# Leftover blocks of a mixture of experts: each down projection moved behind the next block's ups and row turns, and the loads past the end of the list put under conditions

## The chip, the cores and the metric

The kernel runs on one core of one Trainium2 chip. A core has engines with queues of their own: PE (TensorE, matrix products and transposes), DVE (VectorE), ACT (ScalarE), POOL (GpSimd) and SP (SyncE, which here only issues transfers), and 16 DMA engines that move data between the chip's memory (HBM) and the on-chip buffers. Engines work through their own instructions in order and wait for each other by semaphores. The metric is the device time of one execution in microseconds (us); a measurement is the median of several.

## The reference, cut to what matters

One layer of a hybrid decoder trunk over 512 tokens of 1024 values: three token mixers in parallel, then a mixture of experts (64 routed experts, 8 for each token, and one shared), all in 32-bit floats. The change touches only the routed experts:

```python
def block_step(acc, inp):
    tok, wt, e = inp                      # up to 128 tokens of one expert
    xb = x_pad[tok]                       # gather the rows
    hb = jax.nn.silu(xb @ w1[e]) * (xb @ w3[e])      # ups: 1024 -> 2 x 256
    yb = (hb @ w2[e]).astype(jnp.float32) * wt[:, None]   # down: 256 -> 1024
    return acc.at[tok].add(yb), None      # add into the tokens' rows
```

## The kernel before

Routing gives every expert a list of tokens. The kernel sorts the lists into blocks. Full pairs of blocks go first, in a nest of conditions of its own (`n_four`, 8 rounds in this input). What is left goes through `block(i)`, one expert's block of up to 128 tokens at a time. The number of such blocks, `n_left`, is known only at run time (9 here), so `block` is written out 96 times, each time inside one more `tc.If(n_left > i)`: every engine compares and falls into the next block, or jumps out of the nest. The order of the instructions on each engine is the order in which the code is written (`tc.manual_schedule()`); the queues run against each other only by semaphores.

One block i, as it stands in the code:

- **Loads (SP).** `load_up` brings the two up matrices of block i+2, 1 MB each, into `ra[i%2]` (L1006, L1008); `load_down` (L1012) brings its down matrix, 1 MB, into `rad[i%2]`. Blocks past the end of the list have an entry too, so the last two blocks load matrices that nobody uses.
- **Ups (PE, L1153 to L1155).** 24 matmuls: the rows and the weights are each split into a rounded part and the rest (`mT_hi`, `mT_lo`; `wh`, `wl`), and three products of four are summed. While they run, ACT (L49) and DVE (L50) split the next block's weights (`split_a`), in four parts; the last part follows the ups.
- **Activation.** ACT's Silu (L1162), DVE's product with the token's weight, `hw` (L1163).
- **Row turns (PE, L1146).** `x_a` transposes the gathered rows `xg` of the next block, and ACT and DVE split them into `mT_hi` and `mT_lo`.
- **Turns of hw (PE, L1278).** `turn_b` transposes `hw`; ACT copies the result into `hb` (L1280).
- **Down (PE, L1288).** `down_b`: 8 matmuls into two banks `py`; DVE scales each half into `y` (L1289).
- **Row numbers.** `ia[i%2]` holds a block's row numbers and weights. `slots` (DVE, L1133) copies them to `sa`, a tile with two buffers, so that POOL may overwrite `ia` for block i+2 (L1118) and gather that block's rows (L1120).
- **Add (POOL, L1191).** `add_a` sends `y` by an indirect transfer that adds it to the rows `sa` of `acc2` in HBM (the trace names it `acc`). A tile that such a transfer reads is free when the transfer has landed.

After the nest, the sum is read back from HBM in four parts on ACT's and SP's queues (L1378), joined with what the first stage had summed (L1379), normalised and written.

Of the kernel before, what the change touches and what calls it, by code (L numbers as in the profile page):

```python
# [9 lines left out]
F32 = mybir.dt.float32  # L10
F32R = mybir.dt.float32r
BF = mybir.dt.bfloat16
I32 = mybir.dt.int32
AF = mybir.ActivationFunctionType
OP = mybir.AluOpType
# [3 lines left out]
IOA = bass.IndirectOffsetOnAxis  # L19

P = 128
D = 1024
S = 512
# [4 lines left out]
E = 64  # L28
# [6 lines left out]
def trunk(ctx, tc, x, c, ada_w, ada_b, norm1, norm2, w_in, conv_a_w, conv_a_b, ln_a_g, ln_a_b,  # L35
# [4 lines left out]
    nc = tc.nc  # L40
    V, A, G, T = nc.vector, nc.scalar, nc.gpsimd, nc.tensor
    dbg = dbg or {}
    x, out = x[0], out[0]
# [33 lines left out]
    h2d = dram.tile([S, D], F32, name="h2d")  # L77

    acc, acc2 = (dram.tile([S, D], F32, name=n) for n in ("acc", "acc2"))
# [12 lines left out]
    hT = (big.tile([P, KT, S], F32R, name="hT_hi"), big.tile([P, KT, S], F32R, name="hT_lo"))  # L92
# [86 lines left out]
    for i in range(4):  # L179
        a = sp.tile([P, KT, 2, 256], F32, name="ada", bufs=3)  # L180
# [84 lines left out]
    xg = shifted(pl[1], 13, "xg", big)  # L265
# [562 lines left out]
    row, ti = hp.tile([P, TT, 8, 2], F32, name="row"), hp.tile([P, TT, 8], I32, name="ti")  # L828
# [3 lines left out]
    def rt(shape, name, dt=F32, bufs=1, tag=None):  # L832
        return hp.tile([P] + shape, dt, name=name, bufs=2 if tag in ("x1", "h2", "tm", "hf2") else bufs, tag=tag or name)
# [102 lines left out]
    for ts in ((0, 1), (2,), (3,)):  # L936
# [7 lines left out]
        for t in ts:  # L944
# [18 lines left out]
            for g2, q in enumerate(halves):  # L963
# [7 lines left out]
                for i in range(4):  # L971
                    k = g2 * 4 + i
# [18 lines left out]
    ew = est.enter_context(tc.tile_pool(name="ew", bufs=1, side="right"))  # L991
# [11 lines left out]
    def load_up(raw, row, j, after=None):  # L1003
        e = nc.sync.value_load(first[0:1, j:j + 1] if row is None else items[0:1, row, j:j + 1], min_val=0, max_val=E - 1)
        up = raw[j % 2]
        i = nc.sync.dma_start(up[:, :2048], w1v[:, ds(e, 1)].rearrange("p e f -> p (e f)"))  # L1006
        sync_after(i, after)
        nc.sync.dma_start(up[:, 2048:], w3v[:, ds(e, 1)].rearrange("p e f -> p (e f)"))  # L1008

    def load_down(raw, row, j):  # L1010
        e = nc.sync.value_load(first[0:1, j:j + 1] if row is None else items[0:1, row, j:j + 1], min_val=0, max_val=E - 1)
        nc.sync.dma_start(raw.rearrange("p (k f) -> p k f", k=2), w2v[:, ds(e, 1)].rearrange("p e k f -> p (e k) f"))  # L1012
# [19 lines left out]
    V.scalar_tensor_tensor(cls[:, 1], svf, 64.5, cls[:, 2], op0=OP.is_lt, op1=OP.mult)  # L1032
    for j in range(2):
        V.tensor_tensor_scan(cum[:, j], ones, cls[:, j], (2.0, 0.0)[j], op0=OP.mult, op1=OP.add)
    nn_, mi = rt([2], "nn_"), rt([3], "mi", I32)
    V.scalar_tensor_tensor(mi[:, 0:1], cum[:, 0, P - 1:], 31.0, cum[:, 1, P - 1:], op0=OP.min, op1=OP.min)
    V.tensor_scalar(mi[:, 1:2], mi[:, 0:1], 1, None, op0=OP.logical_shift_right)
    V.tensor_scalar(nn_[:, 0:1], mi[:, 1:2], 2.0, None, op0=OP.mult)
# [8 lines left out]
    V.tensor_tensor(L[:, 0], cls[:, 2], lf[:, 0], op=OP.subtract)  # L1047
    V.tensor_tensor_scan(cl_, ones[:, 0:1].to_broadcast([P, 2 * P]), L.rearrange("p a e -> p (a e)"), nn_[:, 1:2], op0=OP.mult, op1=OP.add)
    V.tensor_copy(mi[:, 2:3], cl_[:, 2 * P - 1:])
    it, jk2, th = rt([5], "it"), rt([2 * P], "jk2", tag="tm"), rt([1], "th")  # L1050
    V.scalar_tensor_tensor(jk2[:, :P], cum[:, 0], iop, ones, op0=OP.is_le, op1=OP.mult, accum_out=it[:, 0:1])
    V.scalar_tensor_tensor(jk2[:, :P], cum[:, 1], iop, ones, op0=OP.is_le, op1=OP.mult, accum_out=it[:, 1:2])
# [22 lines left out]
    items = ew.tile([1, 7, P], I32, name="items")  # L1075
    iv = items[:, 0:6].rearrange("o (b a) e -> o a b e", a=2)
    V.memset(items[:, 6], 0)
    for a, src in enumerate((v_, c_)):
# [1 line left out]
        for j in range(3):  # L1080
            T.matmul(ips[:, j], src[:, j:j + 1], ident, start=True, stop=True)
        V.tensor_copy(iv[:, a], ips)
    V.tensor_copy(items[:, 6, 0:2], mi[0:1, 1:3])
    hst.close()
    rawst.close()


    n_four = nc.values_load(items[0:1, 6, 0:1], min_val=0, max_val=15)
    n_left = nc.values_load(items[0:1, 6, 1:2], min_val=0, max_val=NL)
    ep = est.enter_context(tc.tile_pool(name="ep", bufs=1))  # L1090
    psx = est.enter_context(tc.tile_pool(name="psx", bufs=1, space=PSUM))
    xg = [ep.tile([P, D], F32, name=f"xg{b}") for b in range(2)]
# [22 lines left out]
    def gather_a(row, j, n=2):  # L1115
        s = j % 2
        cl = G.value_load(items[0:1, row + 1, j:j + 1], min_val=0, max_val=4 * E - 1)
        G.tensor_copy(ia[s], idxw[:, ds(cl, 2)])  # L1118
        for b in range(n):
            G.indirect_dma_start(out=xg[b], out_offset=None, in_=h2d, in_offset=IOA(ap=ia[s][:, b, 0:1], axis=0),  # L1120
                                 bounds_check=S - 1, oob_is_err=False)

    def gather_c(row, j):
        s = j % 2
# [6 lines left out]
    def slots(src, shape, name):  # L1131
        t = ep.tile([P] + shape, I32, name=name, bufs=2)
        V.tensor_copy(t, src)  # L1133
        return t

    def split_a(j, u, up=None):
        if u < 4:
            src = (up or ra[j % 2]).rearrange("p (z k f) -> p k z f", z=2, k=KT)[:, 2 * u:2 * u + 2]
            split(*(w[u].rearrange("p (k z f) -> p k z f", k=2, z=2) for w in (wh, wl)), src)
        else:  # L1140
            split(wh[u], wl[u], rad[j % 2][:, (u - 4) * 1024:(u - 3) * 1024])

    def x_a(b, g):
        pt = psx.tile([P, 4, P], F32, name="pt", bufs=2)
        for k in range(4):
            T.transpose(pt[:, k], xg[b][:, (g * 4 + k) * P:(g * 4 + k + 1) * P], ident)  # L1146
        split(h2T[0][b][:, g * 4:g * 4 + 4], h2T[1][b][:, g * 4:g * 4 + 4], pt)
# [42 lines left out]
    def add_a(y, at, beside=None, to=acc):  # L1190
        st = G.indirect_dma_start(out=to, out_offset=IOA(ap=at, axis=0), in_=y, in_offset=None,  # L1191
                                  compute_op=OP.add, bounds_check=S - 1, oob_is_err=False)
        g = beside or f"run {st.ins.name}"
        if beside:
            tc.declare_no_dep(st.ins, group=g, reason="the rows of a run are distinct")
        tc.add_to_no_dep_group(g, st.ins)
        return g
# [77 lines left out]
    def turn_b(hw):  # L1275
        p3 = pse.tile([P, 2, 2, P], F32, name="p3")
        for k in range(2):
            T.transpose(p3[:, 0, k], hw[:, k * P:(k + 1) * P], ident)  # L1278
        hb = ew.tile([P, 2, P], F32, name="hb", tag="hh")
        A.activation(hb, p3[:, 0], AF.Copy)  # L1280
        return hb

    def down_b(i, hb):
        y = ew.tile([P, D], F32, name="y", bufs=2)
        for h in range(2):
            py, q = pse.tile([P, 512], F32, name="py", bufs=2), slice(h * 512, h * 512 + 512)
            for k in range(2):
                T.matmul(py, hb[:, k], rad[i % 2][:, k * 1024 + h * 512:k * 1024 + h * 512 + 512], start=(k == 0), stop=(k == 1))  # L1288
            V.tensor_tensor(y[:, q], py, gm2[:, q], op=OP.mult)  # L1289
        return y  # L1290

    def block(i):
        if i:
            load_up(ra, GL, i + 2)
        up = rc[0] if i == 1 else None
        ph = ps_up((0,))
        for u in range(4):
            up_a(ph, u)
            if u < 3:
                split_a(i + 1, u, up)  # L1300
        hw = act_a(ph[0], ia[i % 2][:, 0, 1:2])
        sa = slots(ia[i % 2], [2, 2], "sa")
        split_a(i + 1, 3, up)
        x_a(0, 0)
        x_a(0, 1)
        hT = turn_b(hw)
        gather_a(GL, i + 2, 1)
        add_a(down_b(i, hT), sa[:, 0, 0:1], to=acc2)
        load_down(rad[i % 2], GL, i + 2)

    gs, tok = rad[1][:, :D], ew.tile([P, TT], I32, name="tok")
    nc.sync.dma_start(gs, modr[3:4].to_broadcast([P, D]))
# [25 lines left out]
    with tc.manual_schedule():  # L1338
        gather_a(GA, 0)
        copied = gather_c(GC, 0)  # L1340
        for t in range(2):
            run = add_a(ysh[t], tok[:, t:t + 1], run)
        load_up(rc, GC, 0, copied)
        load_down(rcd, GC, 0)
        for g in range(4):
            x_a(g // 2, g % 2)
        gather_a(GA, 1)
        nc.sync.dma_start(fn[0:1], final_norm[None, :])
        A.activation(gm2, gs, AF.Copy)
        for z in range(2):  # L1350
            zq = slice(z * CH, z * CH + CH)
            A.activation(gm2c[zq], gs[zq, z * 512:z * 512 + 512], AF.Copy)
        for t in range(2, TT):
            run = add_a(ysh[t], tok[:, t:t + 1], run)
        for u in range(6):
            split_a(0, u)
        load_down(rad[1], GA, 1)
        with ExitStack() as nest:
            for i in range(15):
                nest.enter_context(tc.If(n_four > i))  # L1360
                pair_of_runs(2 * i)
                pair_of_runs(2 * i + 1)

        nc.scalar.dma_start(rc[1].rearrange("p (t d) -> p t d", t=TT), acc.rearrange("(t p) d -> p t d", p=P))
        for h in range(2):
            py, q = pse.tile([P, 512], F32, name="py", bufs=2), slice(h * 512, h * 512 + 512)
            T.matmul(py, ones[0:1], fn[0:1, q], start=True, stop=True)
            A.activation(fn[:, q], py, AF.Copy)
        with ExitStack() as nest:  # L1369
            for i in range(NL):  # L1370
                nest.enter_context(tc.If(n_left > i))
                block(i)


    fs = ew.tile([P, TT], F32, name="fs")
# [41 lines left out]
```

## Time and profile before

| | before |
|---|---|
| median of 3 runs | 1465.79 us (1462.84 to 1471.63) |
| the profiled execution | 1467.86 us, span 1466.1 us |
| mean granted clock of PE | 0.966 of full speed |
| leftover stage | first up 1328.65, last `y` ends 1437.9, reads of the sum from 1445.6 |
| distance of one leftover block from the next | 11.86 us |

All times of the profile count from the start of the span. The span is what lies between the first and the last instruction; the execution's time is 1.8 us longer. A row of a timeline gives start, length, engine, line, operation and tiles, and in square brackets how long the engine stood idle before it and what ended that. `PEld` is the loading of a matmul's fixed operand, which overlaps PE; a `q` behind an engine's name stands for its sequencer (branches, semaphores, issuing of transfers).

### The profile page before, as it was taken

What the parts mean: (1) busy time and instruction counts of PE and PEld (TensorE: products, weight loads), DVE (VectorE), ACT (ScalarE), POOL (GpSimd) and SP (SyncE); (2) the same over time, 40 slices, a digit from 0 to 9 for tenths busy, and PEclk for the clock granted to TensorE, in tenths of its full rate; (3) what the DMA queues carried; (4) which work ended last, traced back from release to release, by engine and by line L of the source; (5) the groups of instructions that cost most, each with busy time, mean ns of one, the idle gap of its engine ahead of it and who ended that gap; (6) DMA issues with size and microseconds to landing.
All of it is one profiled execution on the core that took longest, in us unless ns stands there. A gap on an engine that the chain in (4) does not pass through costs nothing. (4 is left out here: it accounts for less than half of the span.)

```text
span 1466.1 us, 24089 instructions
## 1 busy us (share of the span) xinstructions
PE 1347.5 (92%) x8982; PEld 968.7 (66%) x8982; DVE 956.0 (65%) x1816; ACT 620.3 (42%) x1019; POOL 264.8 (18%) x255
## 2 busy tenths in 40 slices
PE   4999999999999979998998978999999999997881
PEld 3877777776766756664686635777677777774660
DVE  6865998987777777233455855666656566564664
ACT  4454334427568658220212213434434443443442
POOL 1000000000000000000000354243342524333332
PEclk8999999999999989999999989999999999999996
DMA  9321231232112117759826348999898989966985
GB/s 339 110 58 31 66 89 47 69 125 92 31 59 80 31 51 237 242 185 333 278 74 238 134 154 266 371 341 322 322 313 294 314 301 337 321 219 206 317 285 208
DMA packets 120634, 289.13 MB, mean 197 GB/s; under 512 B 14883, under 2 KB 68397, under 8 KB 109486
## 3 DMA queue, kind: packets, MB, share of 16 engines
q1 hardware_dynamic: 99266, 242.87, 46.2%
q0 software_dynamic: 17904, 36.01, 10.0%
q10 hardware_dynamic: 3324, 8.49, 1.6%
q8 instruction: 75, 1.23, 0.3%
q14 instruction: 65, 0.53, 0.1%
HBM read 260.24 MB, written 46.97 MB: 210 GB/s over the span
## 5 line engine op out<-in xcount | busy, mean ns | idle before, releaser
L53 PE MATMUL ps_in<-hT_hi,w_hi 128*128 128x512 f32 x496 | 203.9, 411 | 2.7 <-ACT hT_hi L49 2.7
L54 PE MATMUL ps_in<-hT_hi,w_lo 128*128 128x512 f32 x496 | 201.5, 406 | 0.3 <-DVE w_lo L50 0.2
L55 PE MATMUL ps_in<-hT_lo,w_hi 128*128 128x512 f32 x496 | 199.9, 406 | 0.0
L50 DVE TENSOR_TENSOR wl<-ra,wh 128x1024 fp32r<-128x1024 f32 x100 | 122.1, 1224 | 115.2 <-ACT wh L49 111.6
L49 ACT ACTIVATE wh<-ra 128x1024 fp32r<-128x1024 f32 x100 | 105.6, 1060 | 127.8 <-PE ph L1155 90.0
L1153 PE MATMUL ph<-wh,mT_hi 128*128 128x512 f32 x328 | 134.5, 410 | 2.3 <-ACT wh L49 2.3
L1154 PE MATMUL ph<-wl,mT_hi 128*128 128x512 f32 x328 | 129.6, 395 | 0.5 <-DVE wl L50 0.5
L1155 PE MATMUL ph<-wh,mT_lo 128*128 128x512 f32 x328 | 129.3, 394 | 0.0
L50 DVE TENSOR_TENSOR w_lo<-w_raw,w_hi 128x1024 fp32r<-128x1024 f32 x76 | 92.5, 1223 | 51.0 <-ACT w_hi L49 50.8
L53 PEld LDWEIGHTS ps_in<-hT_hi,w_hi 128*128 128x128 f32 x496 | 94.6, 191 | 34.3 <-issue 7.6
L1191 POOL DMA_INDIRECT acc<-y,sa x41 | 65.6, 1599 | 272.9 <-DVE hc L1227 238.0
L54 PEld LDWEIGHTS ps_in<-hT_hi,w_lo 128*128 128x128 f32 x496 | 94.4, 190 | 21.7 <-issue 1.7
L55 PEld LDWEIGHTS ps_in<-hT_lo,w_hi 128*128 128x128 f32 x496 | 94.3, 190 | 21.8 <-issue 2.7
L49 ACT ACTIVATE w_hi<-w_raw 128x1024 fp32r<-128x1024 f32 x76 | 79.3, 1052 | 38.8 <-PE ps_p L55 18.3
L594 DVE SCALAR_TENSOR_TENSOR u<-ut,par,u 128x512 f32<-128x512 f32 x120 | 84.2, 747 | 0.6
L70 POOL TENSOR_TENSOR h<-h,mhalf 128x4 f32<-128x4 f32 x8 | 10.5, 1310 | 358.4 <-DVE h L393 358.4
L1153 PEld LDWEIGHTS ph<-wh,mT_hi 128*128 128x128 f32 x328 | 62.7, 191 | 18.2 <-issue 3.4
L1154 PEld LDWEIGHTS ph<-wl,mT_hi 128*128 128x128 f32 x328 | 62.8, 191 | 15.3 <-issue 1.9
L1155 PEld LDWEIGHTS ph<-wh,mT_lo 128*128 128x128 f32 x328 | 62.6, 191 | 13.3
L1187 DVE TENSOR_TENSOR y<-py,rows 128x512 f32<-128x512 f32 x64 | 44.1, 689 | 31.9 <-PE py L1185 25.1
L49 ACT ACTIVATE wh<-rad 128x1024 fp32r<-128x1024 f32 x34 | 34.1, 1050 | 71.8 <-issue 36.1
L1120 POOL DMA_INDIRECT xg<-h2d,ia x45 | 56.3, 1250 | 20.3 <-issue 8.8
(523 smaller groups left out, 2754.5 us busy)
## 6 DMA issues: line engine op xcount, KB each, us to landing
ra<-in_exp_w_dram SPq DMA_DIRECT2D x52, 1024.0 KB
rc<-in_exp_w_dram SPq DMA_DIRECT2D x34, 1024.0 KB
w_raw<-in_w_in_dram SPq DMA_DIRECT2D x31, 1024.0 KB
rad<-in_exp_w_dram SPq DMA_DIRECT2D x27, 1024.0 KB
adar<-in_ada_w_dram SPq DMA_DIRECT2D x32, 512.0 KB
rcd<-in_exp_w_dram SPq DMA_DIRECT2D x16, 1024.0 KB
ada<-in_ada_w_dram SPq DMA_DIRECT2D x8, 1024.0 KB
gd<-sg SPq DMA_DIRECT2D x24, 256.0 KB
```

Of the source, the lines that this page charges most:

```text
L49: A.activation(hi, src, AF.Copy)
L50: (lo_engine or V).tensor_tensor(lo, src, hi.bitcast(F32), op=OP.subtract)
L53: T.matmul(ps, l[0], r[0], start=first, stop=False)
L54: T.matmul(ps, l[1], r[0], start=False, stop=False)
L55: T.matmul(ps, l[0], r[1], start=False, stop=last)
L594: V.scalar_tensor_tensor(u[:, ct], ut[ct][:, w:w + S], col("caw", w * 4 + ct), u[:, ct], op0=OP.mult, op1=OP.add)
L1120: G.indirect_dma_start(out=xg[b], out_offset=None, in_=h2d, in_offset=IOA(ap=ia[s][:, b, 0:1], axis=0), bounds_check=S - 1, oob_is_err=False)
L1153: T.matmul(ph[b], h2T[0][b][:, k], wh[u][:, q], start=(k == 0), stop=False)
L1154: T.matmul(ph[b], h2T[0][b][:, k], wl[u][:, q], start=False, stop=False)
L1155: T.matmul(ph[b], h2T[1][b][:, k], wh[u][:, q], start=False, stop=(k == KT - 1))
L1187: V.tensor_tensor(y[:, q], py, gate[:, q], op=OP.mult)
L1191: st = G.indirect_dma_start(out=to, out_offset=IOA(ap=at, axis=0), in_=y, in_offset=None, compute_op=OP.add, bounds_check=S - 1, oob_is_er ...
```

## The change

The down projection of block i-1 is written behind the ups and the row turns of block i, ahead of block i's own turns. The turned `hw` therefore lives on from one block to the next, in a fixed tile `hbk` (a part of `xc`, which the stage does not use otherwise). The row numbers are copied into two fixed tiles `sb`. The gather for block i+2 is issued ahead of that down and its add. The last block's down and add come behind the nest, in one of two conditions (whether `n_left` is odd or even decides which `rad` and `sb` they use); three small DVE operations and two register loads on every engine make these flags. Loads of blocks i+2 (ups) and i+1 (down) stand under conditions of their own, so the 6 MB past the end of the list are not loaded.

```diff
-    nn_, mi = rt([2], "nn_"), rt([3], "mi", I32)
+    nn_, mi = rt([2], "nn_"), rt([6], "mi", I32)
...
+    V.tensor_scalar(mi[:, 5:6], mi[:, 2:3], 1, None, op0=OP.logical_shift_right)
+    V.scalar_tensor_tensor(mi[:, 3:4], mi[:, 5:6], -2.0, cl_[:, 2 * P - 1:], op0=OP.mult, op1=OP.add)
+    V.scalar_tensor_tensor(mi[:, 4:5], cl_[:, 2 * P - 1:], 0.5, mi[:, 3:4], op0=OP.is_gt, op1=OP.subtract)
...
-    V.tensor_copy(items[:, 6, 0:2], mi[0:1, 1:3])
+    V.tensor_copy(items[:, 6, 0:4], mi[0:1, 1:5])
...
+    last_even, last_odd = (nc.values_load(items[0:1, 6, i:i + 1], min_val=0, max_val=1) for i in (2, 3))
...
+    def gather_rows(row, j):
+        s = j % 2
+        cl = G.value_load(items[0:1, row + 1, j:j + 1], min_val=0, max_val=4 * E - 1)
+        G.tensor_copy(ia[s], idxw[:, ds(cl, 2)])
+        return lambda: G.indirect_dma_start(out=xg[0], out_offset=None, in_=h2d, in_offset=IOA(ap=ia[s][:, 0, 0:1], axis=0),
+                                            bounds_check=S - 1, oob_is_err=False)
...
-        hb = ew.tile([P, 2, P], F32, name="hb", tag="hh")
-        A.activation(hb, p3[:, 0], AF.Copy)
-        return hb
-
-    def down_b(i, hb):
+        A.activation(hbk, p3[:, 0], AF.Copy)
+
+    def down_b(i):
...
-                T.matmul(py, hb[:, k], rad[i % 2][:, k * 1024 + h * 512:k * 1024 + h * 512 + 512], start=(k == 0), stop=(k == 1))
+                T.matmul(py, hbk[:, k], rad[i % 2][:, k * 1024 + h * 512:k * 1024 + h * 512 + 512], start=(k == 0), stop=(k == 1))
...
     def block(i):
         if i:
-            load_up(ra, GL, i + 2)
+            with tc.If(n_left > i + 2):
+                load_up(ra, GL, i + 2)
...
         hw = act_a(ph[0], ia[i % 2][:, 0, 1:2])
-        sa = slots(ia[i % 2], [2, 2], "sa")
+        V.tensor_copy(sb[i % 2], ia[i % 2])
         split_a(i + 1, 3, up)
+        gather = gather_rows(GL, i + 2)
         x_a(0, 0)
         x_a(0, 1)
-        hT = turn_b(hw)
-        gather_a(GL, i + 2, 1)
-        add_a(down_b(i, hT), sa[:, 0, 0:1], to=acc2)
-        load_down(rad[i % 2], GL, i + 2)
+        gather()
+        if i:
+            add_a(down_b(i - 1), sb[(i - 1) % 2][:, 0, 0:1], to=acc2)
+            with tc.If(n_left > i + 1):
+                load_down(rad[(i - 1) % 2], GL, i + 1)
+        turn_b(hw)
+
+    hbk, sb = xc.rearrange("p (a k s) -> p a k s", a=2, k=2)[:, 0], [ep.tile([P, 2, 2], I32, name=f"sb{i}") for i in range(2)]
...
                 block(i)
+        for z, last in enumerate((last_even, last_odd)):
+            with tc.If(last > 0):
+                add_a(down_b(z), sb[z][:, 0, 0:1], to=acc2)
```

What that does to the order on the engines, at three places. A number behind a tile's name is its buffer, `xN` counts equal instructions, and in brackets stand the semaphores that an instruction waits for (`DMASW` ones are raised by POOL's indirect transfers).

DVE in a block within the stage, before, from the product `hw` on:

```order
L1163 SCALAR_TENSOR_TENSOR hw<-hw,ia_7954,ph 128x256 [waits Activation_49,Pool_49]
L1133 COPY sa<-ia_7954 128x4 [waits DMASW0_49]
L50 TENSOR_TENSOR wl_8074<-ra_7750,wh_8068 128x1024 [waits Activation_49]
L50 TENSOR_TENSOR mT_lo_5784<-pt,mT_hi_5782 128x512 [waits Activation_49] x2
L1289 TENSOR_TENSOR y<-py,rows_8077 128x512 [waits PE_49] x2
```

and after:

```order
L1175 SCALAR_TENSOR_TENSOR hw<-hw,ia_7985,ph 128x256 [waits Activation_49,Pool_49]
L1314 COPY sb_7989<-ia_7985 128x4 [waits DMASW1_49]
L50 TENSOR_TENSOR wl_8107<-ra_7750,wh_8101 128x1024 [waits Activation_49]
L50 TENSOR_TENSOR mT_lo_5784<-pt,mT_hi_5782 128x512 [waits Activation_49] x2
L1299 TENSOR_TENSOR y<-py,rows_8110 128x512 [waits PE_49] x2
```

The rows stand alike; what has moved is what they belong to. The `y` of the second piece are those of the block before, and so is the add that follows them. The copy of block i waits in both for the add of block i-2, the last reader of the tile it overwrites: that add was issued in block i-2 before, and is issued in block i-1 after.

PE from the row turns to the first up of the next block, before:

```order
L1146 MATMUL pt<-ident,xg_7935 128x128 [waits PE_49]
L1146 MATMUL pt<-ident,xg_7935 128x128 x3
L1278 MATMUL p_16242<-ident,hw 128x128 [waits DVE_49]
L1278 MATMUL p_16242<-ident,hw 128x128
L1288 MATMUL py<-rad_7753,hb 128x512 [waits DMAHW1_49,DMAHW5_49,DMAHW0_49,Activation_49]
L1288 MATMUL py<-rad_7753,hb 128x512 x3
L1369 COMPARE_AND_BRANCH
L1153 MATMUL ph<-wh_8065,mT_hi_5782 128x512
```

and after:

```order
L1158 MATMUL pt<-ident,xg_7966 128x128 [waits PE_49]
L1158 MATMUL pt<-ident,xg_7966 128x128 x3
L1298 MATMUL py<-rad_7753,xc 128x512 [waits DMAHW1_49,DMAHW0_49,DMAHW5_49,DVE_49,Activation_49]
L1298 MATMUL py<-rad_7753,xc 128x512
L1298 MATMUL py<-rad_7753,xc 128x512 [waits DVE_49]
L1298 MATMUL py<-rad_7753,xc 128x512
L1322 COMPARE_AND_BRANCH
L1322 UNCONDITIONAL_BRANCH x2
L1290 MATMUL p_16391<-ident,hw 128x128 [waits DVE_49]
L1290 MATMUL p_16391<-ident,hw 128x128
L1386 COMPARE_AND_BRANCH
```

The down (of the block before, from `hbk` in `xc`) stands between the row turns and the turns of `hw`, and two jumps have come in behind it.

DVE at the end of the nest, after: the last `y` inside it, the way out, and the last block's `y`:

```order
L1299 TENSOR_TENSOR y<-py,rows_8110 128x512 [waits PE_49] x2
L1322 UNCONDITIONAL_BRANCH
L1386 UNCONDITIONAL_BRANCH
L1386 UNCONDITIONAL_BRANCH [waits DVE_49] x96
L1094 TENSOR_LOAD items
L1391 COMPARE_AND_BRANCH
L1299 TENSOR_TENSOR y<-py,rows_8110 128x512 [waits DMASW3_49,DMASW4_49,DMASW2_49,DMASW6_49,DMASW0_49,DMASW7_49,DVE_49,PE_49]
L1299 TENSOR_TENSOR y<-py,rows_8110 128x512 [waits PE_49]
```

Before, the nest ended with the last block's own `y`, and what followed on DVE was the joining of the sum (L1379). Now a pair of `y` stands behind the way out, and it waits for the semaphores of POOL's transfers, which POOL counts back on its own way out, once they have landed.

## Rows read from the trace of the kernel before

**Rows 1.** The head of the page: the span, and busy time, share and instructions of each engine.

```profile
span 1466.1 us, 24089 instructions
PE 1347.5 (92%) x8982; PEld 968.7 (66%) x8982; DVE 956.0 (65%) x1816; ACT 620.3 (42%) x1019; POOL 264.8 (18%) x255
```

**Rows 2.** Stretches of the span (start:end and length, then each engine's busy time and instructions, PE's granted clock as a share of full speed, the DMA engines' busy share, GB/s): the start of the stage, three periods within it, and the time from the last down to the reads.

```profile
core 0: us, PE busy (x) PEld busy (x) DVE busy (x) ACT busy (x) POOL busy (x), PEclk, DMA share, GB/s
1325.00:1335.00 10.00, 9.95 (x25) 6.20 (x26) 1.85 (x2) 3.49 (x5) 0.00 (x0) 0.66 0.47 134
...
1347.60:1359.50 11.90, 10.54 (x44) 7.12 (x43) 7.91 (x11) 5.77 (x8) 3.77 (x3) 1.00 0.96 339
...
1395.00:1406.80 11.80, 10.44 (x43) 7.07 (x42) 7.82 (x10) 5.78 (x8) 3.77 (x3) 1.00 0.73 266
1406.80:1418.70 11.90, 10.54 (x44) 7.09 (x43) 7.89 (x11) 5.77 (x8) 3.78 (x3) 1.00 0.85 283
...
1437.20:1445.60 8.40, 0.00 (x0) 0.00 (x0) 0.69 (x1) 0.00 (x0) 1.59 (x1) 0.74 0.39 134
```

**Rows 3.** What engines waited for between 1335.7 and 1437.3 (engine, what it was to do, what it waited for: us in all, times, longest).

```profile
POOL ia L1118 <- DVE sa L1133: 48.6, 9, 12.9
...
ACT wh L49 <- DMA ra<-in_exp_w_dram: 21.5, 4, 5.7
...
PE py L1288 <- ACT hb L1280: 6.7, 9, 0.8
PE p L1278 <- DVE hw L1163: 5.6, 9, 0.6
```

**Rows 4.** The timeline of one block (the second of the nine), from its row turns to the end of the next block's ups.

```profile
1347.62 1.03 PE L1146 MATMUL pt<-ident,xg 128*128 128x128 f32 x8
...
1349.14 0.16 DVE L1133 COPY sa<-ia 128x4 int32<-128x4 int32 x1
1349.21 1.22 DVE L50 TENSOR_TENSOR wl<-rc,wh 128x1024 fp32r<-128x1024 f32 x1
...
1349.28 0.44 PE L1278 MATMUL p<-ident,hw 128*128 128x128 f32 x2 [0.62 <-DVE hw L1163]
...
1350.34 1.28 DVE L50 TENSOR_TENSOR mT_lo<-pt,mT_hi 128x512 fp32r<-128x512 f32 x2
...
1350.45 3.70 PE L1288 MATMUL py<-rad,hb 128*128 128x512 f32 x8 [0.74 <-ACT hb L1280]
1350.74 1.08 POOL L1120 DMA_INDIRECT xg<-h2d,ia  x1 [0.27 <-POOL ia L1118]
...
1353.59 0.80 PE L1153 MATMUL ph<-wh,mT_hi 128*128 128x512 f32 x1
...
1354.19 0.69 DVE L1289 TENSOR_TENSOR y<-py,rows 128x512 f32<-128x512 f32 x1 [1.02 <-PE py L1288]
...
1354.23 0.39 PE L1154 MATMUL ph<-wl,mT_hi 128*128 128x512 f32 x1
...
1355.16 1.58 POOL L1191 DMA_INDIRECT acc<-y,sa  x1 [3.34 <-DVE y L1289]
...
1359.23 0.39 PE L1155 MATMUL ph<-wh,mT_lo 128*128 128x512 f32 x1
```

**Rows 5.** DVE's copies of the row numbers, all nine: shortest, median and longest in ns, first and last start.

```profile
L1133 DVE COPY sa<-ia x9: 158/163/164, 1337.3 to 1432.2; 128x4 int32<-128x4 int32 x9
```

**Rows 6.** The timelines of SP and of POOL around the add of the sixth block: the three loads of its time, the add, and the gather after it.

```profile
1401.55 0.38 SPq L1012 DMA_DIRECT2D rad<-in_exp_w_dram  x1
1402.87 0.33 SPq L1006 DMA_DIRECT2D ra<-in_exp_w_dram  x1
1403.42 0.34 SPq L1008 DMA_DIRECT2D ra<-in_exp_w_dram  x1
...
1402.52 1.58 POOL L1191 DMA_INDIRECT acc<-y,sa  x1 [3.33 <-DVE y L1289]
...
1409.95 1.08 POOL L1120 DMA_INDIRECT xg<-h2d,ia  x1 [0.27 <-POOL ia L1118]
```

**Rows 7.** The packets of POOL's queue (q0: packets, MB, share of 16 engines) in 1411.5 to 1412.5, and in 1412.5 to 1413.5.

```profile
q0 software_dynamic: 82, 0.03, 20.4%
...
q0 software_dynamic: 32, 0.00, 1.8%
```

**Rows 8.** Adds with few or no loads beside them: the last add ahead of the stage and the read that waits for it, and the last add of the stage and the first reads of the sum.

```profile
1323.13 1.58 POOL L1238 DMA_INDIRECT acc<-yc,sc__12185  x1 [0.30 <-issue]
...
1330.20 0.38 ACTq L1364 DMA_DIRECT2D rc<-acc  x1
...
1438.17 1.59 POOL L1191 DMA_INDIRECT acc<-y,sa  x1 [3.34 <-DVE y L1289]
1445.62 0.97 ACTq L1378 DMA_DIRECT2D rc<-acc  x2
```

**Rows 9.** Ways out of a nest: PE's first matmuls behind the nest of the fours (its exit is L1358) and its first ups, and SP's wait at the exit from the leftover nest (L1369).

```profile
1325.05 3.67 PE L1367 MATMUL py<-rows,ones 1*128 1x512 f32 x4 [5.05 <-DVEq L1358]
...
1329.24 0.63 PE L1154 MATMUL ph<-wl,mT_hi 128*128 128x512 f32 x1
1329.67 0.63 PE L1155 MATMUL ph<-wh,mT_lo 128*128 128x512 f32 x1
...
SPq L1369 <- SPq L1369: 5.7, 1, 5.7
```

## Prediction

> **What bounds the kernel now.** I read the page first, and it misleads: over the span PE is busy 92% [rows 1], as if only fewer matmuls could help. The change touches one stage, the nine leftover blocks, so I cut that stretch into its periods [rows 2]. There PE is busy 10.4 to 10.5 of 11.8 us at full clock while the DMA engines run at 0.73 to 0.96: two resources near their limits. The waits of the stage [rows 3] say what PE lacks: 5.6 us in 9 waits for `hw` and 6.7 in 9 for `hb`, 1.36 us a block. No other wait there holds up the ups: ACT's 21.5 us for loads are four waits in its own idle time. The timeline of one block [rows 4] shows where the two stand: the row turns end, 0.62 us pass until DVE's product `hw`, the turns L1278 run, 0.74 us pass until ACT's copy `hb`, then the down projection. Without these waits PE needs 11.86 - 1.36 = 10.5 us; ends are modelled and overlap the next start (the first up stands at 1353.59, within the 3.70 us of the downs), so I take 10.3. The period, 11.86, is the distance of the copies L1133, (1432.2 - 1337.3)/8 [rows 5].
>
> **The change, part by part.** *Down projection and turns.* With the previous block's down behind the row turns, `hw` and `hbk` have 3.7 us of matmuls as cover. The two waits go: 1.56 us a block (11.86 - 10.3), for eight blocks 12.5 if nothing else is late.
>
> *What is late next.* The add moves with its down: the add of block i-1 now goes out in block i. DVE's copy of the indices does not move with it. In block i it overwrites `sb[i%2]`, from which the add of block i-2 took its row numbers, and it waits until that add has landed (first pair of pieces of the order). Before, the same copy waited for an add issued two blocks back, 17.7 us earlier in [rows 4, 5] (1355.16 to the copy two blocks on, 1349.14 + 2 × 11.86 = 1372.86); no copy waited. Now the add is issued within the block before, and the copy follows within one period. Call D the start of the copy. Behind it DVE has the last weight split, two splits of the turned rows and the two `y` [rows 4]: from the copy to the end of the splits 1351.62 - 1349.14 = 2.48, two `y` of 0.69 are 1.38, and the add starts 0.28 after `y` (1354.88 to 1355.16). So the next add stands at D + 4.15, and the next copy waits for its landing. If L is the time from issue to landing, **the period is 4.15 + L, or PE's 10.3 if that is longer**: the wait binds from L = 6.2. PE, ACT and POOL queue behind it: the third up of the next block needs the split rows, POOL's copy `ia` and the gather wait for `sb` (as POOL does today, 48.6 us in [rows 3]), and SP's next load into `ra` waits for the weight split.
>
> *The size of L.* No row is this case, so it has bounds. Above: the add of 1402.52 has its three loads around it, `rad` 0.97 us before, `ra` 0.35 and 0.90 after [rows 6]. Its last 4 KB rows are moved in 1411.5 to 1412.5, small packets of its queue follow until 1413.5 (the gather of 1409.95 fetches one row, the last block has one token) [rows 7]: L is 10 to 11, I take 10.8. Below: where no load runs, the add of 1323.13 is over by 1330.20, when the read that waits for it is issued, and the last one, of 1438.17, by 1445.62 [rows 8]: at most 7.1 and 7.45; 6.5 is my value for an add alone. In between: an add beside loads ends nearly with them. After the change `rad` is issued near D, the two `ra` at about D + 1.5 and D + 2, the add at D + 4.15: against its loads it stands some 3 us later than before. If it still ends with them, L = 10.8 - 3 = 7.8. It can't fall much below, since the gather now goes out in the 3 us ahead of the add on the same queue (before 4.4, 1350.74 to 1355.16). I take 7.8: **a period of 11.95, where it was 11.86.** The waits on PE are replaced by one on DVE of the same size.
>
> The Trainium skill, "DMA: Bandwidth & Descriptors", section "Anatomy of one DMA — SWDGE (gpsimd) path", fits such a transfer at 2.0 us + bytes/436e3, an estimate of 3.2 us for 512 KB. By that the wait would never bind, and it is the second rival below. The trace speaks against it: 10 us beside loads.
>
> *Sum.* **Start:** block 0 has no down in it. Its copy stands at 1337.3 as before; the third up of block 1 waits for the first row split, about 2.1 later, and 22 more ups of 0.227 (1354.23 to 1359.23) end at 1344.4; D1 = 1345.9 with a free `sb`. The add of block 0 goes out at 1350.05, with its loads around it as before, so L = 10.8 and D2 = 1360.9; before, 1337.3 + 2 × 11.86 = 1361.0. The 3 us that PE had won are gone: -0.1. **Middle:** D2 to D7, 5 × (11.95 - 11.86) = +0.5. **Block 7 to 8:** the ups of a block 9 are not loaded any more, so the add of block 6 has one load of three beside it: 4.15 + 6.5 = 10.65, so -1.2. The left-out 6 MB are worth this and no more: before, too, nothing waits for the surplus loads at the end.
>
> **End:** before, from D8 to the reads of the sum, 1432.2 to 1445.6 = 13.4. After, all engines leave the nest first, and the last down and its add come behind it. The add of block 7 is issued at D8 + 4.15 and lands 6.5 later; POOL counts its semaphores back only then, DVE's first `y` of block 8 waits for POOL there (third piece of the order), two `y` and the way to the add are 1.7: add at D8 + 12.4, landed 18.9: +5.5. PE also leaves by a jump; the exit from the nest of the fours cost PE 5.05 us and the last one SP 5.7 [rows 9]. Behind that idle stretch the granted clock was 0.66 over 1325 to 1335 [rows 2], and the ups stood 0.43 apart instead of 0.227. PE is through with its turns at about D8 + 3.2 and out of the nest 5.05 later. If the last down then runs at half rate, it takes 7.4 instead of 3.7 us and it, not POOL, sets the last add: 8.3 + 7.4 + 0.7 + 0.3 = D8 + 16.7, landed 23.2, +10. I take +7, between the two. The exit's jumps themselves are paid before, too.
>
> New work is small: three tiny DVE operations and two register loads ahead of the stage, and two conditions a block on every engine. On PE, DVE and ACT they stand behind queued work; on SP they stand ahead of loads that aren't late; on POOL ahead of the copy that waits anyway. A block's condition that holds costs nothing visible today (ups follow downs without a gap, [rows 4]).
>
> The sum is -0.1 + 0.5 - 1.2 + 7 = **+6 us** against the profiled 1467.9, which is 2.1 above the median of the runs; carried to the median, **1472 us**.
>
> **The rivals.** *The add stays slow* (slower): L remains 10.8, as every add beside loads shows. For it: a later add still has up to 10 us of loads ahead of it, and the gather just before it. Against: the longer the period, the more of it is free of loads. Period 14.95: 5 × 3.1 = 15.5, sum +21, 1487 us. It decides (over 0.5%, 7.3 us) from L = 8.1.
>
> *The wait does not bind* (faster): adds land within 6.2, as for an add alone, and PE sets the pace. For it: the loads are issued earlier than the add. Against: [rows 7]. D2 would be 1345.9 + 10.3 = 1356.2 (-4.8), five periods and the last 6 × 1.56 = -9.4, the end +5.5 to +7: -7 to -9, 1457 to 1459 us.
>
> *The conditions cost a jump each.* The nests' exits took 5.05 and 5.7 us [rows 9], and in the changed kernel every condition that holds ends in a jump over its short other arm. If each took 5 us, PE (two a block, one of them with 3.7 us of downs queued ahead of it) would lose some 5 us a block, +40 us, 1510. Against it: the targets are a few instructions away, those of the exits a whole nest. The Trainium skill, "Runtime: NRT & Kernel Launch", section "Instruction fetch mechanics", says that a taken branch whose target lies outside the fetched window stops its engine until the page is there; the exits agree, and no row shows a short jump.
>
> **How the numbers follow.** My forecast, L from 7 to 8.1, has 0.5; the slow add 0.32; the wait that does not bind 0.14; the jumps 0.04. The range reaches from 1458, where PE sets the pace, to 1483, L = 10: about 0.8. Of 0.5% (7.3 us, what a measurement of this kernel can tell from no change) the forecast's own range, 1467 to 1474, lies nearly all within; an end at full clock keeps it there, one at half rate with L = 8 puts it over. So faster 0.1, same 0.5, slower 0.4.
>
> **What would show it.** Right: DVE's copy `sb` has idle time ahead of it, 2 to 4 us in six or seven blocks, ended by the landing of an add; PE's waits for `hw` and `hb` are gone and a wait for the split rows has come; copies 11.5 to 12.5 apart; block 1's row turns start near 1344.4; from the last copy to the reads 18 to 24 us. Wrong: copies at 10.3 without idle ahead (L below 6.2), or at 14 and more. I would also be wrong if a load for `ra` came late, since SP now waits for a split behind the copy: ACT would then wait for `ra` with PE behind it.

## The result, and the profile after

The changed kernel takes 1480.65 us (median of 5 runs, 1478.31 to 1482.93) against 1466.11 (5 runs, 1462.84 to 1471.63); the ratio of the runs is 1.0069, with a 95% interval from 1.0043 to 1.0095. It is slower: 0.69% is above the 0.5% that was called no change, though the interval begins at 0.43%. The page of its profiled execution, head and busy times:

```profile
span 1481.0 us, 24285 instructions
PE 1355.5 (92%) x8982; PEld 974.5 (66%) x8982; DVE 956.3 (65%) x1819; ACT 622.2 (42%) x1019; POOL 264.5 (18%) x255
```

Against [rows 1] the span is 14.9 us longer with the same 8982 matmuls; PE's busy time has grown by 8.0, at a mean granted clock of 0.959 instead of 0.966, and the share says 92% in both. The stage again has to be cut out. First DVE's copies of the row numbers, now into `sb` (all nine: shortest, median, longest in ns, first and last start; below, the idle time of DVE just ahead of them):

```profile
L1314 DVE COPY sb<-ia x9: 163/170/172, 1338.7 to 1445.3; 128x4 int32<-128x4 int32 x9
  DMA acc<-y,sb: 23.8, 6
```

In [rows 5] nine copies span 94.9 us; now it is 1445.3 - 1338.7 = 106.6, and 23.8 us of it DVE stands idle in front of six of them until an add has landed. Before, no copy waited. What engines waited for in the stage (1330 to 1455):

```profile
POOL ia L1131 <- DVE sb L1314: 76.1, 9, 13.7
...
DVE sb L1314 <- DMA acc<-y,sb: 23.8, 6, 6.5
...
PE ph L1167 <- DVE mT_lo L50: 11.4, 4, 4.4
...
PE pt L1158 <- DMA xg<-h2d,ia: 6.4, 4, 2.9
...
PE p L1290 <- DVE hw L1175: 0.6, 1, 0.6
```

Against [rows 3], PE's waits for `hw` and `hb`, 12.3 us together, are down to 0.6. In their place PE waits 11.4 us for the split rows and 6.4 for a gather, and POOL waits 76.1 instead of 48.6 for DVE's copy. The timeline of DVE around one copy, and POOL's adds on both sides of it:

```profile
1388.76 0.47 DVE L1175 SCALAR_TENSOR_TENSOR hw<-hw,ia,ph 128x256 f32<-128x256 f32 x1
1395.76 0.17 DVE L1314 COPY sb<-ia 128x4 int32<-128x4 int32 x1 [6.53 <-DMA acc<-y,sb]
1395.83 1.22 DVE L50 TENSOR_TENSOR wl<-ra,wh 128x1024 fp32r<-128x1024 f32 x1
1396.97 1.28 DVE L50 TENSOR_TENSOR mT_lo<-pt,mT_hi 128x512 fp32r<-128x512 f32 x2
1398.17 1.28 DVE L1299 TENSOR_TENSOR y<-py,rows 128x512 f32<-128x512 f32 x2
...
1384.53 1.60 POOL L1203 DMA_INDIRECT acc<-y,sb  x1 [1.28 <-DVE y L1299]
1399.73 1.58 POOL L1203 DMA_INDIRECT acc<-y,sb  x1 [1.30 <-DVE y L1299]
```

This is the loop: the add of 1384.53 has landed at 1395.7, 11.2 us later; the copy, the last weight split, two row splits and two `y` take until 1399.45; the next add goes out at 1399.73, 3.97 us behind the copy. The stretches from one such copy to the next:

```profile
core 0: us, PE busy (x) PEld busy (x) DVE busy (x) ACT busy (x) POOL busy (x), PEclk, DMA share, GB/s
...
1338.70:1347.30 8.60, 6.46 (x26) 4.55 (x26) 6.47 (x10) 5.75 (x8) 2.12 (x2) 1.00 0.72 272
1347.30:1366.70 19.40, 16.61 (x62) 10.97 (x62) 8.14 (x12) 7.46 (x11) 3.76 (x3) 0.91 0.65 208
1366.70:1380.60 13.90, 10.28 (x36) 7.26 (x37) 7.75 (x11) 5.60 (x7) 3.75 (x3) 0.88 0.79 260
1380.60:1395.80 15.20, 12.28 (x49) 7.61 (x47) 7.75 (x11) 6.27 (x9) 3.78 (x3) 1.00 0.81 265
1395.80:1409.30 13.50, 10.08 (x34) 7.51 (x35) 7.74 (x11) 5.60 (x7) 3.74 (x3) 0.75 0.84 269
1409.30:1423.40 14.10, 12.80 (x51) 8.15 (x49) 7.70 (x11) 6.27 (x9) 3.76 (x3) 1.00 0.64 233
1423.40:1433.50 10.10, 8.20 (x32) 6.59 (x33) 7.61 (x10) 4.45 (x6) 3.75 (x3) 0.83 0.42 121
...
```

The first period takes 8.6 us, with no down in it, the second 19.4, and four of 13.5 to 15.2 follow, where [rows 2, 5] have 11.86. The DMA engines are busier in the periods of [rows 2] (0.73 to 0.96) than now (0.64 to 0.84 in those four). Only when the loads run out does a period fall to 10.1, the last but one, and the last is 11.7 (1433.53 to 1445.27).

### The profile page after: what moved, and what is told of

It is laid out like the page before. It is cut to its first block, busy times and chain, and to the rows that moved or that the text cites. A ratio compares the mean times of both kernels' runs of the same rounds, so it can differ in the third digit from the quotient of the medians.

```text
span 1481.0 us, 24285 instructions
## 1 busy us (share of the span) xinstructions
PE 1355.5 (92%) x8982; PEld 974.5 (66%) x8982; DVE 956.3 (65%) x1819; ACT 622.2 (42%) x1019; POOL 264.5 (18%) x255
## 5 line engine op out<-in xcount | busy, mean ns | idle before, releaser
L1167 PE MATMUL ph<-wh,mT_lo 128*128 128x512 f32 x328 | 132.2, 403 | 11.5 <-DVE mT_lo L50 11.4
L1203 POOL DMA_INDIRECT acc<-y,sa x32 | 51.2, 1601 | 241.8 <-DVE hc L1239 236.9
L1165 PEld LDWEIGHTS ph<-wh,mT_hi 128*128 128x128 f32 x328 | 64.1, 195 | 16.9 <-ACT wh L49 2.5
L70 POOL TENSOR_TENSOR h<-h,mhalf 128x4 f32<-128x4 f32 x8 | 10.5, 1310 | 359.3 <-DVE h L393 359.3
L49 ACT ACTIVATE wh<-rad 128x1024 fp32r<-128x1024 f32 x34 | 34.1, 1051 | 71.8 <-issue 36.1
L50 DVE TENSOR_TENSOR mT_lo<-pt,mT_hi 128x512 fp32r<-128x512 f32 x86 | 55.5, 686 | 6.3 <-ACT mT_hi L49 5.8
```

Source lines behind the costliest of these rows:

```text
L49: A.activation(hi, src, AF.Copy)
L50: (lo_engine or V).tensor_tensor(lo, src, hi.bitcast(F32), op=OP.subtract)
L1165: T.matmul(ph[b], h2T[0][b][:, k], wh[u][:, q], start=(k == 0), stop=False)
L1167: T.matmul(ph[b], h2T[1][b][:, k], wh[u][:, q], start=False, stop=(k == KT - 1))
```

## Experiments

Each theory's expectations were written down before the runs. The theory: DVE's copy waits for an add that is now issued only one block ahead and is slow beside loads. Rivals: the order of the loads or the jumps of the new conditions set the period. The kernel before took 1459.21 us on the chip of the first four runs and 1469.52 on that of the other three (in the profiles of these runs the first copy stands anywhere from 1327.0 to 1341.7), so a time counts by its difference to that, and the distance of the copies most of all.

### Four tiles for the row numbers

```diff
-        V.tensor_copy(sb[i % 2], ia[i % 2])
+        V.tensor_copy(sb[i % 4], ia[i % 2])
+        V.tensor_copy(sf[i % 2], ia[i % 2])
...
-            add_a(down_b(i - 1), sb[(i - 1) % 2][:, 0, 0:1], to=acc2)
+            add_a(down_b(i - 1), sb[(i - 1) % 4][:, 0, 0:1], to=acc2)
...
-                add_a(down_b(z), sb[z][:, 0, 0:1], to=acc2)
+                add_a(down_b(z), sf[z][:, 0, 0:1], to=acc2)
...
```

> The changed kernel with four tiles sb in turn instead of two (and two more, sf, only for the last block's add behind the nest), so that DVE's copy overwrites row numbers whose add went out three blocks earlier. Theory (the copy's wait for the add of the block before sets the period): DVE no longer waits for a landing, the copies stand 10.5 to 12 us apart instead of 13.5 to 15.2, bounded next by the gather, which takes 5 to 9 us beside loads; 1463 to 1470 us. Rival (the order of the loads and the jumps of the conditions set the period, the wait only fills it): copies stay 13.5 or more apart, 1478 to 1482 us.

Measured: 1460.2 us against 1459.21 for the kernel before on this chip, ratio 0.9989 (0.9955 to 1.0022). The loss is gone. The copies, and one of their periods as a stretch:

```profile
L1314 DVE COPY sb<-ia x9: 158/161/165, 1327.0 to 1415.0; 128x4 int32<-128x4 int32 x9
...
1371.00:1382.00 11.00, 10.61 (x48) 7.68 (x49) 7.38 (x12) 5.37 (x8) 3.74 (x3) 1.00 0.94 308
```

They are (1415.0 - 1327.0)/8 = 11.0 us apart, none waits for anything, and the DMA engines are back at 0.94. The wait was the loss; the rival falls. Of the gain that the two waits on PE promised, 0.86 of 1.56 us a block is there; some of the rest goes into PE's waits for a gather, three in all. The end takes half of the 8 × 0.86 us back, 16.9 us from the last copy to the reads of the sum (1431.89) instead of 13.4, so the time is that of the kernel before and not better.

### The same wait in the old order

```diff
-        sa = slots(ia[i % 2], [2, 2], "sa")
+        V.tensor_copy(sone, ia[i % 2])
+        sa = sone
...
+    sone = ep.tile([P, 2, 2], I32, name="sone")
```

> The kernel before with one tile for the copied row numbers in the leftover stage instead of two: the same wait, one block deep, in the old order and without any condition on the loads. Theory: the copy of block i waits for the add of block i-1, which goes out 6.0 us after that block's copy, so the period is 6.0 + L, 16 to 17 us with L = 10 to 10.9; 8 periods, about +35 to +40 us, 1500 to 1508 us. Rival (the wait alone does not set the pace): within 5 us of the kernel before.

Measured: one run of 1486.76 us beside 1459.21, +27.6.

```profile
L1302 DVE COPY sone<-ia x9: 156/170/170, 1331.6 to 1449.0; 128x4 int32<-128x4 int32 x9
  DMA acc<-y,sone: 36.1, 8
```

All eight later copies wait, 36.1 us together, and stand (1449.0 - 1331.6)/8 = 14.7 apart. So the wait alone, without the new order and without a condition, makes the loss. My 16 to 17 were too high, since an add goes out not 6.0 but in five of seven blocks 4.0 us behind a copy that waited: the down projection does not wait for the copy and is mostly done by then.

### No loads for the ups

```diff
-        if i:
-            with tc.If(n_left > i + 2):
-                load_up(ra, GL, i + 2)
```

> The changed kernel without the loads of the ups in the leftover stage (two of three MB a block; the blocks compute with old weights). Theory: L is long because loads run beside the add; here adds land 6 to 7 us after their issue, the period falls to 10.3 to 11, about 1455 to 1460 us. Rival (L is the add's own time, rows and receipts): L stays 9 to 11, periods 13 or more, 1476 to 1482 us.

Measured: one run of 1450.28 us, 8.9 less than the median of the kernel before, whose fastest run took 1452.01.

```profile
L1311 DVE COPY sb<-ia x9: 161/169/170, 1329.8 to 1412.5; 128x4 int32<-128x4 int32 x9
  DMA acc<-y,sb: 9.7, 6
```

Copies (1412.5 - 1329.8)/8 = 10.3 apart, with waits of 9.7 us in all instead of 23.8. With one load of three left, the six adds that a copy waits for take 6.3 to 7.8 us from issue to that copy, 6.9 on the mean, which is fast enough for PE to set the pace, at the 10.3 that I had taken as PE's need. The length of an add beside loads is the loads'.

### No gathers

```diff
-        gather()
```

> The changed kernel without the gathers of the leftover stage (the blocks compute with old rows). It asks what keeps an add at 10 us though it goes out after its loads. If it is the gather just ahead of it in the same queue: L falls to 7 or 8, periods of 11 to 12, 1465 to 1471 us. If the loads alone do it: L stays 9.5 to 11, periods of 13.5 to 15, 1476 to 1481 us.

Measured: one run of 1467.59 us, 8.4 more than the median of the kernel before but within its runs (up to 1467.88), so only the copies tell something:

```profile
L1314 DVE COPY sb<-ia x9: 161/170/172, 1332.0 to 1430.3; 128x4 int32<-128x4 int32 x9
  DMA acc<-y,sb: 21.5, 6
```

From the first to the last pass 98.3 us, 8.3 less than with gathers. 4.4 of these come at the start: the first add stands 12.6 us behind the first copy (1344.53) instead of 17.0, as the row turns of the second block have no gather to wait for. The adds beside loads still take 9.6 us on the mean of five until the copy that they release, against 10.4 with gathers, and DVE's idle time is nearly what it was. So the gather ahead of an add in its queue is worth 0.8 us of L; neither expectation was met whole, but it is the loads that make L long.

This run shows one thing more. With the gathers gone, POOL's queue (q0) carries the adds alone, and what they move can be read beside the loads (q1). The add of 1398.77, from its issue to the copy that it releases (1408.39):

```profile
q1 hardware_dynamic: 507, 2.93, 79.9%
q0 software_dynamic: 144, 0.07, 4.3%
```

The five adds move 0.32, 0.32, 0.46, 0.41 and 0.07 MB and take 10.9, 9.7, 9.7, 8.1 and 9.6 us; beside them the loads move 3.06, 2.08, 2.18, 1.75 and 2.93 MB. The smallest add is no faster than the others: none of its packets is moved before 1403.0, while the loads keep the engines full (a share of 1.03 from 1398.7 on). So the length of an add does not follow its own bytes here.

### The conditions alone, and the new order without them

The kernel before with the conditions on its loads:

```diff
-            load_up(ra, GL, i + 2)
+            with tc.If(n_left > i + 2):
+                load_up(ra, GL, i + 2)
...
-        load_down(rad[i % 2], GL, i + 2)
+        with tc.If(n_left > i + 2):
+            load_down(rad[i % 2], GL, i + 2)
```

> The kernel before with nothing but the conditions on the loads (loads of block i+2 only where the list has one): the second part of the change alone. Theory: the jumps over the other arms are short and hidden, the left-out loads were not waited for except that the last add lands a little sooner: 1462 to 1467 us, ratio to before 0.997 to 1.001. Rival (a condition costs a jump that an engine waits for): 8 blocks of 0.5 us or more, 1470 us and above.

Measured: 1467.19 us against 1469.52, ratio 0.9988 (0.9971 to 1.0005). Together, two conditions a block on every engine and the loads that they leave out change nothing that can be measured. That need not mean that each is worth nothing: in the profiled run two periods are longer (14.1 and 12.4 us), and the end is shorter, 11.2 us from the last copy to the reads instead of 13.4. Whether the conditions make those two periods was not tested.

And the changed kernel without them:

> The changed kernel with the loads unconditional: the reordering alone. Theory (the wait for the add, beside loads): the last two or three adds have loads beside them again and wait longer, 3 to 4 us each, 1485 to 1492 us. Rival (the conditions cost the time): faster than the changed kernel, 1466 to 1475 us.

Measured: 1496.53 us against 1469.52, ratio 1.0170 (1.0132 to 1.0209): slower than the changed kernel, by more than I had written: it loses 27.0 us to the kernel before, the changed kernel 14.5.

```profile
L1313 DVE COPY sb<-ia x9: 164/170/171, 1341.7 to 1456.3; 128x4 int32<-128x4 int32 x9
  DMA acc<-y,sb: 33.6, 7
```

With loads beside them to the end, seven copies wait, 33.6 us together, and the copies stand 14.3 apart on the mean. So in this order leaving the surplus loads out shortens the time: it frees the last adds of loads. The rival of the jumps is gone on both sides: with the conditions alone there is no loss, and without them it is larger.

### No recent transfer in anyone's way

POOL writes the row numbers into a ring of eight tiles `il`, from which the adds read directly, and the gather goes out at the start of the block, into the other tile `xg` (a cut; the two comments stand only here):

```diff
...
+        gather_rows(GL, i + 2)            # into il[(i + 2) % 8], rows into xg[(i + 1) % 2]
         up = rc[0] if i == 1 else None
...
-        V.tensor_copy(sb[i % 2], ia[i % 2])
+        V.tensor_copy(sf[i % 2], il[i % 8])   # for the last block alone
         split_a(i + 1, 3, up)
-        gather = gather_rows(GL, i + 2)
-        x_a(0, 0)
-        x_a(0, 1)
-        gather()
+        x_a(0, 0, i % 2)
+        x_a(0, 1, i % 2)
...
-            add_a(down_b(i - 1), sb[(i - 1) % 2][:, 0, 0:1], to=acc2)
+            add_a(down_b(i - 1), il[(i - 1) % 8][:, 0, 0:1], to=acc2)
...
```

> The changed kernel with the row numbers in a ring of eight tiles that POOL fills directly (no copy on DVE for the adds inside the nest), and the gather for block i+2 issued at the start of block i into the other of the two tiles xg. Neither the copy nor the row turns then wait for a recent transfer. Theory: PE or the loads set the pace, row turns 10.2 to 11 us apart, block 1's near 1345; the end costs 2 us more than before: 1453 to 1461 us, faster than both. Rival (loads, not the waits, set the pace at 11.8 or more): 1466 us and above.

Measured: 1457.24 us against 1469.52, ratio 0.9926 (0.9899 to 0.9954): faster than the kernel before, by 0.74%, with 0.46% as the least of the interval. Its copies for the last block (those of the blocks 0, 1 and 8, whose numbers lie in the tiles `ia`), and three stretches of 10.4 or 10.5 us:

```profile
L1314 DVE COPY sf<-ia x3: 161/163/165, 1333.6 to 1417.2; 128x4 int32<-128x4 int32 x3
...
1354.50:1365.00 10.50, 10.50 (x45) 7.18 (x44) 6.28 (x9) 5.53 (x8) 2.85 (x3) 1.00 0.95 319
1365.00:1375.40 10.40, 9.51 (x41) 6.53 (x40) 5.15 (x8) 4.04 (x6) 2.86 (x3) 1.00 0.98 365
...
1385.90:1396.30 10.40, 9.81 (x42) 6.75 (x41) 6.89 (x11) 4.93 (x8) 2.86 (x3) 1.00 0.97 329
```

The period is (1417.2 - 1333.6)/8 = 10.45, PE's need of 10.3 and a little; the DMA engines run at 0.95 to 1.00 in the four periods from 1354.5 on. Both resources are near their limits, and the gain that the change was able to bring is there: 8 × (11.86 - 10.45) = 11.3 us in the periods. The end takes some of it back, 16.7 us from the last copy to the reads (1433.91) instead of 13.4. The ring and the early gather went in together, so this run does not tell what each is worth.

## Why the prediction was right, and where it was not

The range, 1458 to 1483, held the 1480.65. The verdict I gave most weight, no change, did not come; it was slower, the 0.4. One of my own signs of being wrong came too, copies "at 14 and more" (14.2 on the mean of four). And that the range held is in part luck: with the measured L of 10.4 and all else as I had it, the sum would have been 6.2 + 5 × 2.6 = +19, 1485 us, above the range. Two terms that I had too large brought it back, each by some 5 us (five long periods, where four came, and the end); the start of the stage, too small by 4.4, took a part of that away. Step by step:

- **The two waits on PE go: right.** 12.3 us became 0.6, and the last experiment shows what that is worth when nothing else is late.
- **The copy waits for an add issued one block back, and the period is 4.15 + L: right as a mechanism.** Six copies waited; the next add stands 3.97 us behind the copy. Four tiles instead of two remove it all, one tile in the old order makes it.
- **L = 7.8: the term that was mis-sized.** From issue to the copy that it releases, the five adds beside loads took 11.0 (1355.67 to 1366.65), 9.9, 11.2, 9.5 and 10.1 us: 10.4 on the mean. That is nearly the first rival's 10.8, and its period of 14.95 stands against a measured 14.2 in the mean of four. I had let the add stand 3 us later against its loads. But the loads themselves hang on the loop. SP's rows:

```profile
1364.81 0.39 SPq L1012 DMA_DIRECT2D rad<-in_exp_w_dram  x1
1368.07 0.34 SPq L1006 DMA_DIRECT2D ra<-in_exp_w_dram  x1
1368.66 0.33 SPq L1008 DMA_DIRECT2D ra<-in_exp_w_dram  x1
1381.86 0.39 SPq L1012 DMA_DIRECT2D rad<-in_exp_w_dram  x1
1383.57 0.34 SPq L1006 DMA_DIRECT2D ra<-in_exp_w_dram  x1
1384.58 0.34 SPq L1008 DMA_DIRECT2D ra<-in_exp_w_dram  x1
```

  The first three stand as far ahead as I had put them or further, 5.8, 2.6 and 2.0 us ahead of their add of 1370.62, and that still took 9.9 us, not 7.8. The next three stand at 2.7 and 1.0 ahead of and with their add of 1384.53, nearer to their places in the kernel before: PE's row turns had waited for a gather until 1377.2, the down came late, and the load of `rad` with it. I had named the gather as a neighbour of the add and not as something that is late itself.
- **Why a longer period does not ease the adds.** My argument against the first rival was that a longer period has more time free of loads. It has, but at the wrong end. Stretches of the kernel after, just ahead of a copy, just behind it, and then beside the add:

```profile
1376.60:1380.50 3.90, 3.27 (x14) 2.08 (x15) 0.34 (x1) 1.36 (x3) 0.00 (x0) 1.00 0.38 85
1380.60:1384.50 3.90, 3.81 (x16) 2.40 (x15) 3.64 (x6) 1.10 (x2) 2.18 (x2) 1.00 0.25 72
1384.60:1390.00 5.40, 5.05 (x26) 3.71 (x25) 4.07 (x4) 4.55 (x7) 1.52 (x1) 1.00 1.01 366
```

  While the end of the add is awaited and until the next one is out, the DMA engines stand at 0.38 and 0.25; then loads, gather and add go out together and the share stands at 1.01, all of the stretch. The wait gathers all transfers into one heap. In two other periods the load of `rad` fills the gap ahead of the copy (0.92 and 0.95), and the L that follows is a shorter one (9.9 and 9.5).
- **D2: -0.1 predicted, +4.3 measured.** From the first to the third copy I had 23.6 us; it took 1366.65 - 1338.66 = 28.0, against 23.7 before. SP's `ra` loads go out at 1340.10 and 1340.71, with the gather of 1340.27. Before, they stood behind the load for the down, 5.0 and 5.7 us after the gather (1343.87 and 1344.59 against 1338.91). Now the gather ran beside them, and block 1's row turns waited for it:

```profile
1348.76 1.94 PE L1158 MATMUL pt<-ident,xg 128*128 128x128 f32 x8 [2.86 <-DMA xg<-h2d,ia]
```

  They started 3 us later than I had put them (1344.4 and the 1.4 that the stage starts later). Behind the wait the granted clock was 0.50 (1348.7 to 1351.0), and row turns and down took 1.9 and 4.2 us where [rows 4] have 1.0 and 3.7; this is most of the rest. SP's move was in the diff, and I did not count what it put beside the gather.
- **The end: +7 predicted, +2.0.** From the last copy to the reads: 15.4 us instead of 13.4.

```profile
1449.25 1.59 POOL L1203 DMA_INDIRECT acc<-y,sb  x1 [1.30 <-DVE y L1299]
1455.84 1.29 DVE L1299 TENSOR_TENSOR y<-py,rows 128x512 f32<-128x512 f32 x2 [6.87 <-DMA acc<-y,sb]
1457.47 1.57 POOL L1203 DMA_INDIRECT acc<-y,sb  x1 [6.64 <-DVEq L1391]
1460.70 0.86 ACTq L1398 DMA_DIRECT2D rc<-acc  x2
```

  The path is the one I named (the add of block 7, POOL, two `y`, the last add, the reads), and its first `y` waited 6.87 us. From the issue of the first add to that `y` pass 6.6 us, as good as the 6.5 I took; what was quicker is the last add, of one row, 3.2 instead of 6.5. [rows 8] had given upper bounds only, 7.1 and 7.45, and 6.5 was my value for any add alone. Whether POOL waited on its way out for this add or for the surplus gather just ahead of it in its queue (1446.89), the trace does not settle: its chain of work names the gather. PE's slower clock came (the last 8 matmuls took 5.17 us, [rows 4] have 3.70) and was hidden behind POOL.
- **The sum.** The first copy 1.4 later (from what lies ahead of the stage), +4.3 to D2, +7.4 to D8 (78.6 instead of 71.2 us), +2.0 at the end, -0.2 behind it: 14.9, the difference of the spans. I had -0.7 for the stretch from D2 to D8: five periods of 11.95 and one of 10.65, where four of 14.2 came, one of 10.2 (no load ran beside the add of 1427.33) and one of 11.7.
- **The jumps: rightly left at a small chance.** The Trainium skill, "Runtime: NRT & Kernel Launch", section "Instruction fetch mechanics", says that a taken branch whose target has not been fetched stalls its engine. The exits agree (SP's 5.2 us here). The short jumps show no such stall that the time would tell: ratio 0.9988 with the conditions alone.

## What to carry to other kernels

When work is moved to a later place, ask which buffers it still reads there and who overwrites them: the tile freed one block later can cost more than the wait that the move removes, and it can be a small one: here it was 2 KB of row numbers, and with four such tiles instead of two the loss was gone. Price such a wait by the slowest landing that the trace shows beside the same loads, since transfers that a late release holds back come out together and can make each other late. Such a loop can show as idle DMA engines just before the wait ends and full ones after it, as in the period shown here; where another load fills the gap, it does not.

## What the runs showed of the hardware

PE's granted clock fell inside the stage, which I had expected only at its end. Rows of PE behind the copy of 1395.76, and two stretches, before and from the first of them:

```profile
1397.71 0.80 PE L1167 MATMUL ph<-wh,mT_lo 128*128 128x512 f32 x1 [4.39 <-DVE mT_lo L50]
1398.30 0.63 PE L1165 MATMUL ph<-wh,mT_hi 128*128 128x512 f32 x1
1398.73 0.63 PE L1166 MATMUL ph<-wl,mT_hi 128*128 128x512 f32 x1
...
1390.50:1397.70 7.20, 2.82 (x9) 1.14 (x8) 1.94 (x4) 0.39 (x1) 1.43 (x2) 0.88 0.96 311
1397.70:1402.00 4.30, 4.29 (x10) 3.42 (x11) 2.78 (x4) 1.06 (x1) 2.31 (x2) 0.50 0.98 357
```

After 4.39 us of idle time the clock stood at 0.50, the lower of its two levels (1.2 of 2.4 GHz), and the ups 0.43 us apart instead of 0.23, as in [rows 9]. In this kernel the add still came last, with 2.46 us of waiting ahead of the next copy. An add of one row with nothing beside it is over at most 3.2 us after its issue (1457.47 to 1460.70); the same kind of transfer took 9.5 to 11.2 beside loads, and in the run without gathers 9.6 where it moved 0.07 MB. The fit that the prediction quoted from the Trainium skill ("DMA: Bandwidth & Descriptors", section "Anatomy of one DMA — SWDGE (gpsimd) path") was worked out for 512 KB, the size of the tile `y`; the five adds of the run without gathers move 0.07 to 0.46 MB, so its 3.2 us and the 3.2 of the one row are not the same thing. By the bytes it would be an estimate of 2.2 us for the add of 0.07 MB; it says nothing of one that shares the engines.
